# An encoder layer on one core: a snapshot copy moved, one pair's weight sums by DMA, and a written order at the second feed-forward's entry

## The chip, the core and the metric

The kernel runs on one core of a Trainium2 chip. The metric is the device time of one execution in microseconds. TensorE (PE) multiplies matrices, VectorE (DVE) and ScalarE (ACT) work on tiles, GpSimd (POOL) does a little of that and starts some of the transfers, and SyncE (SP) starts the others. Each engine works through its own queue in order and waits where an operand or a buffer is not ready.

## The reference

One layer of an encoder over 512 tokens and 16 meta tokens, 1024 features wide: a feed-forward (FF), a mixer of two branches (a state-space branch and a sparse attention), and a second FF, each with a norm ahead of it and one behind it. `D_FF` is 2816.

```python
def swiglu(x, w_gate, w_up, w_down):
    return (jax.nn.silu(x @ w_gate) * (x @ w_up)) @ w_down
...
        hn = rms_norm(h, ff1_norm_pre[l])
        h = h + 0.5 * rms_norm(swiglu(hn, ff1_w_gate[l], ff1_w_up[l], ff1_w_down[l]), ff1_norm_post[l])
        ...
        merged = g[:, :, 0] * (y_a @ w_branch_a[l]) + g[:, :, 1] * (y_b @ w_branch_b[l])
        h = h + rms_norm(merged @ w_out[l], mix_norm_post[l])
        hn = rms_norm(h, ff2_norm_pre[l])
        h = h + 0.5 * rms_norm(swiglu(hn, ff2_w_gate[l], ff2_w_up[l], ff2_w_down[l]), ff2_norm_post[l])
```

All of it is in float32 outside; the change lies in the last two lines.

## The kernel before

**Products.** Every float32 operand is split into two fp16 halves, high and low: ACT copies the high half (scaled), DVE subtracts it from the operand for the low half. A float32 product is three fp16 matmuls: high by high, high by low, low by high. `split` (L293 on ACT, L295 on DVE) does it for activations; `unit` (L272, L273) for a tile of weights `ws`, whose halves are `wh`.

**Second FF.** The input is `hf`, 8 tiles of 128 features by 512 tokens, both halves. It comes from `wout`, which for each block of 128 tokens multiplies by `w_out` (reading `mg`), norms the rows (tiles `y` of pool W) and in `wout_T` has PE transpose them and `split` write `hf`. Block 0 comes last. The first 256 of the FF's columns are done plainly: `prod(j, 128, SEQ)` for three blocks, and `prod(j, 0, 128)`, 96 matmuls, once block 0's `hf` is there; silu, times up, `split` into `h2f` (L1559, L1560, L295).

The other 2560 columns are worked by class `Strassen` in ten pairs p = 0 to 9 of 128 + 128 columns for gate and for up. A pair is one 2x2 block product in seven block products instead of eight, 24 matmuls of 128x256 each (L139). Its operands are four raw quadrants of the weights (`raw`, 128x4x512 float32, by DMA from a layout that the host made), of which three are split into `wr`, and four sums of quadrants (`sums`, DVE, L122 to L124: slots 0 and 1 are quadrant 3 plus quadrant 0 or 1; slot 2 is slot 0 plus quadrant 1; slot 3 is slot 2 plus quadrant 2), split into `whs` (L112 and L117). The other factor is `hf` itself or one of four combinations of it (`comb` in float32, split into `tops`), made for 128 token columns at a time.

**Order inside a pair.** Products 1, 2, 6, 5, 7 of pair p + 1 and products 4 and 3 of pair p alternate (`run`). Bank Y of a pair collects products 1, 6, 7 and 4 one on another, and between them ACT takes snapshots: p1 after product 1, u2 after 6, u3 after 7 (L155; they read the running sum, so the next product into that bank waits for the copy). `conversions(p)` gives six steps that make the halves of pair p + 2's weights, and `run` calls them by `c()` between the products; the fifth makes the high half `whs` of the second weight and stands ahead of product 7 and of u3.

**What sets the order.** `run` is under a manual schedule: PE, DVE and ACT take its instructions in the written order. The entry ahead of it is ordered by a list scheduler with priorities; `with self.after(marks)` holds what stands in it behind two instructions of `wout`. There pair 0 is loaded and its halves are made. The pools of `wout` close, and those of the second FF (`KP`, `CP`; `tops` lies in `CP`) open behind that; a tile of the new pool is first written when the old pool's readers are through. The constant `ACC` is 0 in the kernel before, and the branch of `load` under it isn't taken.

Of the kernel before, what the change touches and what calls it, by code (L numbers as in the profile page):

```python
# [19 lines left out]
SEQ = 512  # L20
# [53 lines left out]
class Strassen:  # L74
# [14 lines left out]
    def load(self, p):  # L89
        l, nc = self.l, self.l.nc  # L90
        with l.hi():
            for i, w in enumerate(self.w):
                r = l.wst.tile([128, 4, 512], F32, tag="ws", name="raw")
                s = l.SG.tile([128, 4, 512], F32, tag="sums", name="sums", bufs=2)
                if ACC:
                    nc.sync.dma_start(r[:, 0:3], w[p, :, 0:3])
                    nc.sync.dma_start(s[:, 0:2], w[p, :, 3:4].to_broadcast([128, 2, 512]))
                    nc.gpsimd.dma_start(s[:, 0:2], w[p, :, 0:2], accum_op=ADD)
                else:
                    nc.sync.dma_start(r, w[p])  # L100
                self.raw[p, i], self.sums[p, i] = r, s
                self.ops[p, i] = (l.SG.tile([128, 2, 3, 512], F16, tag="wr", name="wr", bufs=4),
                                  l.whl.tile([128, 2, 4, 512], F16, tag="wh", name="whs"))

    def conversions(self, p):

        l, nc = self.l, self.l.nc
        v, s = nc.vector, nc.scalar

        def hi(i, b):  # L110
            src = (self.raw, self.sums)[b][p, i]
            s.activation(self.ops[p, i][b][:, 0], src[:, 0:3] if b == 0 else src, AF.Copy, scale=WS)  # L112

        def lo(i, b):
            src = (self.raw, self.sums)[b][p, i]
            o = self.ops[p, i][b]
            v.scalar_tensor_tensor(o[:, 1], src[:, 0:3] if b == 0 else src, WS, o[:, 0], op0=MUL, op1=SUB)  # L117

        def add(i):
            r, t = self.raw[p, i], self.sums[p, i]  # L120
            if not ACC:
                v.tensor_add(t[:, 0:2], r[:, 3:4].to_broadcast([128, 2, 512]), r[:, 0:2])  # L122
            v.tensor_add(t[:, 2], t[:, 0], r[:, 1])
            v.tensor_add(t[:, 3], t[:, 2], r[:, 2])  # L124
# [16 lines left out]
    def run(self, CP, moving, pair):  # L141
# [16 lines left out]
        for p in range(-1, self.n):  # L158
# [50 lines left out]
            c()  # L209
            if n_:  # L210
                prod(p + 1, 7, Y, "ps", False)
                copy(p + 1, "u3")
                v.scalar_tensor_tensor(st[p + 1, "C"][:, 2], st[p + 1, "u3"], -1.0, by(Z[p + 1]), op0=MUL, op1=SUB)
# [7 lines left out]
class Layer:  # L221
# [1277 lines left out]
    def ff2(self):  # L1499
# [9 lines left out]
        with self.after(self.wout_marks[0]):  # L1509
            sg.load(0)  # L1510
            for f in sg.conversions(0):
                f()
# [11 lines left out]
        for _ in self.wout_T(0):  # L1524
            pass
# [16 lines left out]
        for c in (1, 0):  # L1542
# [3 lines left out]
            for dst, (k, t) in ((b12, (0, 1)), (b22, (1, 1)), (b11, (0, 0)), (b21, (1, 0))):  # L1546
                v.tensor_add(dst, q[k][t][0][:, :, cs], q[k][t][1][:, :, cs])
            v.tensor_sub(t3, b22, b12)
            v.scalar_tensor_tensor(n2, t3, -1.0, b11, op0=MUL, op1=SUB)
            v.scalar_tensor_tensor(t4, n2, -1.0, b21, op0=MUL, op1=SUB)  # L1550
            v.tensor_sub(n1, b11, b12)
            for i, x in ((1, n2), (0, n1), (2, t3), (3, t4)):
                self.split(ops[:, 0, i, :, cs], ops[:, 1, i, :, cs], x)
        for j in range(2):
            prod(j, 0, 128)
        t_ = pair(0, 1)
        for j in range(2):
            sl = CP.tile([128, SEQ], F32, tag="C", name="sl2", bufs=2)
            s.activation(sl, pgs[j][0], AF.Silu, scale=IWS)  # L1559
            v.scalar_tensor_tensor(sl, pgs[j][1], IWS, sl, op0=MUL, op1=MUL)  # L1560
            self.split(t_[:, 0, j], t_[:, 1, j], sl)
        T = lambda i: [ops[:, x, i] for x in range(2)]
        moving = {1: q[0][0], 2: q[1][0], 3: q[1][1], 4: T(3), 5: T(0), 6: T(1), 7: T(2)}
        with self.tc.manual_schedule(engines={mybir.EngineType.PE, mybir.EngineType.DVE, mybir.EngineType.Activation}):
# [93 lines left out]
ACC = 0  # L1658
# [35 lines left out]
```

## Time and profile before

| | |
|---|---|
| runs | 1118.3, 1121.31, 1120.45 us; median 1120.45 us |
| profiled execution | 1121.73 us, span 1120.0 us |
| mean granted clock of PE | 0.979 of full speed |
| PE busy | 1050.3 us (94%), 8382 matmuls |
| DVE, ACT, POOL busy | 759.9 us (68%), 469.5 us (42%), 171.8 us (15%) |
| second FF in the trace | entry 759 to 812 us, loop 812 to 972 us, down projection behind it to the end |

Times are us from the span's start. A matmul's end is modelled, so the steps from start to start are the better measure of a product. The granted clock is a share of 2.4 GHz; 0.5 is 1.2 GHz.

### The profile page before, as it was taken

The numbers are of one execution on the slowest core, as the hardware profiler recorded it, in microseconds if no ns is written. First come the engines' busy times: TensorE is split into PE (matmuls) and PEld (weight loads), VectorE is DVE, ScalarE is ACT, GpSimd is POOL, SyncE is SP. The second block draws the span as 40 slices with busy tenths as digits, with TensorE's granted clock in tenths as the row PEclk, the third lists the DMA queues.
The fourth block names the chain that finished last, engine by engine and source line by source line (L and its number), as shares of the span: only waits on it lengthen the run. The fifth ranks groups of instructions, "written<-read, shape, count | busy, mean of one in ns | idle before, by whom it ended". The sixth has DMA issues, their size and how long they took to land.

```text
span 1120.0 us, 20553 instructions
## 1 busy us (share of the span) xinstructions
PE 1050.3 (94%) x8382; PEld 792.5 (71%) x8382; DVE 759.9 (68%) x1644; ACT 469.5 (42%) x855; POOL 171.8 (15%) x258
## 2 busy tenths in 40 slices
PE   7899999999999999789998899998799899899997
PEld 5788888888888888676654456665688788774443
DVE  7558776668323585599977976599978888754222
ACT  6444333223222155555656453334545445532200
POOL 4400133310000231046431323100000000000000
PEclk9999999999999999999998999999989999999999
DMA  6764445433424045956323124130323323446111
GB/s 193 161 217 135 136 152 168 145 119 111 136 82 118 1 138 170 263 163 171 115 71 110 53 88 163 39 114 38 124 103 114 114 78 111 127 153 225 41 38 38
DMA packets 94479, 135.38 MB, mean 121 GB/s; under 512 B 17336, under 2 KB 69192, under 8 KB 91824
## 3 DMA queue, kind: packets, MB, share of 16 engines
q1 hardware_dynamic: 88704, 119.92, 34.2%
q0 software_dynamic: 5056, 13.08, 4.1%
q8 instruction: 66, 1.08, 0.4%
q10 hardware_dynamic: 624, 1.06, 0.3%
q14 instruction: 29, 0.24, 0.1%
HBM read 118.45 MB, written 19.05 MB: 123 GB/s over the span
## 4 chain that ended last, share of the span: by engine, by line
PE 71%; DVE 14%; DMA 5%; issue 4%; ACT 3%; POOL 1%; SPq 1%; DVEq 0%; ACTq 0%; POOLq 0%
PE psps L316 10%; PE psps L312 10%; PE psps L314 10%; PE psps L139 8%; PE scps L312 6%; PE scps L314 6%; PE scps L316 6%; PE ptps L139 4%; DVE wh L273 3%; DMA ws<-in_w_in_dram 2%; PE avps L139 2%; DMA ws<-in_ff_w_up_dram 1%; DMA X<-in_x_dram 1%; ACT wh L272 1%; PE ptps L316 1%
## 5 line engine op out<-in xcount | busy, mean ns | idle before, releaser
L273 DVE SCALAR_TENSOR_TENSOR wh<-ws,wh 128x512 f16<-128x512 f32 (+2 forms) x184 | 171.9, 972 | 103.1 <-ACT wh L272 102.7
L316 PEld LDWEIGHTS <-wh 128*128 128x128 f16 x1616 | 160.3, 99 | 47.3 <-issue 5.9
L314 PEld LDWEIGHTS <-wh 128*128 128x128 f16 x1616 | 160.6, 99 | 43.2 <-issue 9.7
L312 PEld LDWEIGHTS <-wh 128*128 128x128 f16 x1616 | 160.1, 100 | 42.4 <-issue 6.4
L272 ACT ACTIVATE wh<-ws 128x512 f16<-128x512 f32 (+2 forms) x184 | 138.5, 815 | 120.2 <-PE scps L316 52.3
L312 PE MATMUL psps<-hn,wh 128*128 128x256 f16 (+2 forms) x640 | 166.0, 301 | 3.8 <-DVE kk L297 1.5
L314 PE MATMUL psps<-hn,wh 128*128 128x256 f16 (+2 forms) x640 | 166.4, 301 | 1.1 <-POOL hn L295 0.6
L316 PE MATMUL psps<-hn,wh 128*128 128x256 f16 (+2 forms) x640 | 166.2, 301 | 0.0
L139 PEld LDWEIGHTS <-whs 128*128 128x128 f16 x960 | 93.9, 98 | 14.6 <-issue 3.6
L139 PEld LDWEIGHTS <-wr 128*128 128x128 f16 x720 | 72.5, 101 | 24.7 <-issue 14.3
L312 PE MATMUL scps<-hn,wh 128*128 128x272 f16 (+1 forms) x344 | 69.8, 279 | 4.7 <-ACT sl L507 4.7
L314 PE MATMUL scps<-hn,wh 128*128 128x272 f16 (+1 forms) x344 | 69.4, 278 | 0.0
L316 PE MATMUL scps<-hn,wh 128*128 128x272 f16 (+1 forms) x344 | 69.3, 278 | 0.0
L139 PE MATMUL psps<-tops,whs 128*128 128x256 f16 x480 | 55.8, 273 | 3.2 <-DVE tops L295 1.8
L112 ACT ACTIVATE whs<-sums 128x2048 f16<-128x2048 f32 x20 | 38.1, 1903 | 38.9 <-DVE sums L124 38.9
L117 DVE SCALAR_TENSOR_TENSOR whs<-sums,whs 128x2048 f16<-128x2048 f32 x20 | 45.7, 2287 | 1.6 <-ACT whs L112 1.6
L139 PE MATMUL psps<-tops,wr 128*128 128x256 f16 x240 | 31.7, 295 | 12.5 <-ACT u L155 12.5
L353 POOL DMA_DIRECT2D g_ff_norm_post<-in_ff_norm_post_dram x1 | 0.6, 572 | 269.3 <-ACT sl L175 269.3
L1360 POOL TENSOR_TENSOR BM<-BV,iacc 128x272 f32<-128x272 f32 (+1 forms) x32 | 28.7, 906 | 85.1 <-DVE asm L1366 73.6
L314 PE MATMUL psps<-h,wh 128*128 128x256 f16 (+1 forms) x176 | 41.5, 276 | 0.0
L316 PE MATMUL scps<-h,wh 128*128 128x256 f16 (+1 forms) x176 | 41.5, 276 | 0.0
L312 PE MATMUL psps<-h,wh 128*128 128x256 f16 (+1 forms) x176 | 41.5, 276 | 0.0
(412 smaller groups left out, 2151.1 us busy)
## 6 DMA issues: line engine op xcount, KB each, us to landing
ws<-in_ff_w_down_dram SPq DMA_DIRECT2D x18, 1024.0 KB, 5.1
ws<-in_w_in_dram SPq DMA_DIRECT2D x14, 1024.0 KB, 6.5
ws<-in_ff_w_gate_dram SPq DMA_DIRECT2D x11, 1024.0 KB, 5.4
ws<-in_ff_w_up_dram SPq DMA_DIRECT2D x11, 1024.0 KB, 5.5
raw<-ff_gate_pairs SPq DMA_DIRECT2D x10, 1024.0 KB, 4.8
raw<-ff_up_pairs SPq DMA_DIRECT2D x10, 1024.0 KB, 4.9
ws<-in_w_out_dram SPq DMA_DIRECT2D x4, 1024.0 KB, 5.1
ws<-in_ff_w_down_dram SPq DMA_DIRECT2D x4, 768.0 KB, 4.6
```

Source lines behind the costliest of these rows:

```text
L112: s.activation(self.ops[p, i][b][:, 0], src[:, 0:3] if b == 0 else src, AF.Copy, scale=WS)
L117: v.scalar_tensor_tensor(o[:, 1], src[:, 0:3] if b == 0 else src, WS, o[:, 0], op0=MUL, op1=SUB)
L139: mm(out, a, b[:, kt], start=first and i == kt == x == 0, stop=kt == 3 and x == 2, skip_group_check=True)
L272: nc.scalar.activation(wt[:, 0, ks], st[:, ks], AF.Copy, scale=WS)
L273: nc.vector.scalar_tensor_tensor(wt[:, 1, ks], st[:, ks], WS, wt[:, 0, ks], op0=MUL, op1=SUB)
L312: mm(p, a[0], bh, start=first, stop=False)
L314: mm(p, a[0], bl, start=False, stop=False)
L316: mm(p, a[1], bh, start=False, stop=last)
L353: self.nc.gpsimd.dma_start(dst, bass.AP(tensor=src.tensor, offset=src.offset, ap=[[0, dst.shape[0]], [1, n]]))
L1360: nc.gpsimd.tensor_add(BM[:, :w], self.BV[:, h, NA - w:], madd[:, f:])
```

## The change

Four edits, all around the second FF. First, `load` builds the sums of the pairs under `ACC`, now 1 (pair 0 alone), by DMA: for each of the two weights SP broadcasts quadrant 3 into all four slots of `sums`, POOL starts seven DMAs of 128x512 that add a quadrant to a slot, and `raw` is loaded without quadrant 3. `add` does nothing for that pair. Second, the steps of pair 1's conversions are dealt out anew. Third, `run` puts product 7 and the copy u3 ahead of the fifth `c()`. Fourth, at the entry `load(0)` is no longer held behind `wout`, and pair 0's halves, `wout_T(0)`, the last combinations of block 0, `prod(j, 0, 128)` and the silu stand in written order.

```diff
--- before.py
+++ after.py
@@ -92,36 +92,42 @@
             for i, w in enumerate(self.w):
                 r = l.wst.tile([128, 4, 512], F32, tag="ws", name="raw")
                 s = l.SG.tile([128, 4, 512], F32, tag="sums", name="sums", bufs=2)
-                if ACC:
+                if p < ACC:
+                    nc.sync.dma_start(s, w[p, :, 3:4].to_broadcast([128, 4, 512]))
                     nc.sync.dma_start(r[:, 0:3], w[p, :, 0:3])
-                    nc.sync.dma_start(s[:, 0:2], w[p, :, 3:4].to_broadcast([128, 2, 512]))
-                    nc.gpsimd.dma_start(s[:, 0:2], w[p, :, 0:2], accum_op=ADD)
+                    for c, q in ((0, 0), (1, 1), (2, 0), (3, 0), (2, 1), (3, 1), (3, 2)):
+                        nc.gpsimd.dma_start(s[:, c], w[p, :, q], accum_op=ADD)
                 else:
                     nc.sync.dma_start(r, w[p])
                 self.raw[p, i], self.sums[p, i] = r, s
                 self.ops[p, i] = (l.SG.tile([128, 2, 3, 512], F16, tag="wr", name="wr", bufs=4),
                                   l.whl.tile([128, 2, 4, 512], F16, tag="wh", name="whs"))
 
+    def hi(self, p, i, b):
+
+        src = (self.raw, self.sums)[b][p, i]
+        self.l.nc.scalar.activation(self.ops[p, i][b][:, 0], src[:, 0:3] if b == 0 else src, AF.Copy, scale=WS)
+
+    def lo(self, p, i, b):
+        src = (self.raw, self.sums)[b][p, i]
+        o = self.ops[p, i][b]
+        self.l.nc.vector.scalar_tensor_tensor(o[:, 1], src[:, 0:3] if b == 0 else src, WS, o[:, 0], op0=MUL, op1=SUB)
+
+    def add(self, p, i):
+        if p < ACC:
+            return
+        v = self.l.nc.vector
+        r, t = self.raw[p, i], self.sums[p, i]
+        v.tensor_add(t[:, 0:2], r[:, 3:4].to_broadcast([128, 2, 512]), r[:, 0:2])
+        v.tensor_add(t[:, 2], t[:, 0], r[:, 1])
+        v.tensor_add(t[:, 3], t[:, 2], r[:, 2])
+
     def conversions(self, p):
 
...
+        hi, lo, add = (lambda *a, f=f: f(p, *a) for f in (self.hi, self.lo, self.add))
+        if p == 1:
+            return [lambda: (hi(0, 0), hi(1, 0), lo(0, 0), lo(1, 0)), lambda: (add(0), hi(0, 1)),
+                    lambda: (add(1), hi(1, 1)), lambda: lo(0, 1), lambda: None, lambda: lo(1, 1)]
         return [lambda: (hi(0, 0), add(0)), lambda: (lo(0, 0), hi(1, 0)), lambda: (lo(1, 0), hi(0, 1)),
                 lambda: (lo(0, 1), add(1)), lambda: hi(1, 1), lambda: lo(1, 1)]
 
@@ -206,10 +212,11 @@
                 h = list(h)
                 s.activation(h[0], slf, AF.Copy)
 
-            c()
             if n_:
                 prod(p + 1, 7, Y, "ps", False)
                 copy(p + 1, "u3")
+            c()
+            if n_:
                 v.scalar_tensor_tensor(st[p + 1, "C"][:, 2], st[p + 1, "u3"], -1.0, by(Z[p + 1]), op0=MUL, op1=SUB)
             if p >= 0:
                 v.tensor_sub(h[1], slf, h[0])
@@ -1506,10 +1513,8 @@
         sg = Strassen(self, [I["ff2_%s_pairs" % k] for k in ("gate", "up")])
 
         ug, uu = [self.unit(w, 0, KT, 0, 256, parts=F2P) for w in (wg, wu)]
-        with self.after(self.wout_marks[0]):
-            sg.load(0)
-            for f in sg.conversions(0):
-                f()
+        sg.load(0)
+        manual = lambda: self.tc.manual_schedule(engines={mybir.EngineType.PE, mybir.EngineType.DVE, mybir.EngineType.Activation})
         pgs = [[self.ps("ps"), self.ps("sc")] for j in range(2)]
 
         def prod(j, a, b):
@@ -1521,8 +1526,14 @@
 
         for j in range(2):
             prod(j, 128, SEQ)
-        for _ in self.wout_T(0):
-            pass
+        with self.after(self.wout_marks[0]), manual():
+            for b in range(2):
+                for i in range(2):
+                    sg.hi(0, i, b)
+                    if b == 0:
+                        sg.lo(0, i, b)
+            for _ in self.wout_T(0):
+                pass
         self.sctx.close()
         self.lctx_close()
         self.kctx, self.cctx = ExitStack(), ExitStack()
@@ -1539,29 +1550,52 @@
         q = [[[hf[i][:, 4 * k:4 * k + 4, 256 * t:256 * t + 256] for i in range(2)] for t in range(2)] for k in range(2)]
         R = [KP.tile([128, 4, 256], F32, tag="h", name="raw", bufs=11) for _ in range(4)]
         Tt = [KP.tile([128, 4, 256], F32, tag="h", name="comb", bufs=11) for _ in range(4)]
-        for c in (1, 0):
+        def combine(c, step):
             cs = slice(128 * c, 128 * c + 128)
             b11, b12, b21, b22 = (x[:, :, cs] for x in R)
             n1, n2, t3, t4 = (x[:, :, cs] for x in Tt)
-            for dst, (k, t) in ((b12, (0, 1)), (b22, (1, 1)), (b11, (0, 0)), (b21, (1, 0))):
+
+            def whole(dst, k, t):
                 v.tensor_add(dst, q[k][t][0][:, :, cs], q[k][t][1][:, :, cs])
-            v.tensor_sub(t3, b22, b12)
-            v.scalar_tensor_tensor(n2, t3, -1.0, b11, op0=MUL, op1=SUB)
-            v.scalar_tensor_tensor(t4, n2, -1.0, b21, op0=MUL, op1=SUB)
-            v.tensor_sub(n1, b11, b12)
-            for i, x in ((1, n2), (0, n1), (2, t3), (3, t4)):
+
+            def split(i, x):
                 self.split(ops[:, 0, i, :, cs], ops[:, 1, i, :, cs], x)
-        for j in range(2):
-            prod(j, 0, 128)
+            if step == 0:
+                whole(b12, 0, 1)
+                whole(b22, 1, 1)
+                v.tensor_sub(t3, b22, b12)
+                split(2, t3)
+            if step == 1:
+                whole(b11, 0, 0)
+                v.scalar_tensor_tensor(n2, t3, -1.0, b11, op0=MUL, op1=SUB)
+                split(1, n2)
+            if step == 2:
+                v.tensor_sub(n1, b11, b12)
+                split(0, n1)
+            if step == 3:
+                whole(b21, 1, 0)
+                v.scalar_tensor_tensor(t4, n2, -1.0, b21, op0=MUL, op1=SUB)
+                split(3, t4)
+        for c, step in ((1, 0), (1, 1), (1, 2), (1, 3), (0, 0)):
+            combine(c, step)
         t_ = pair(0, 1)
-        for j in range(2):
-            sl = CP.tile([128, SEQ], F32, tag="C", name="sl2", bufs=2)
-            s.activation(sl, pgs[j][0], AF.Silu, scale=IWS)
-            v.scalar_tensor_tensor(sl, pgs[j][1], IWS, sl, op0=MUL, op1=MUL)
-            self.split(t_[:, 0, j], t_[:, 1, j], sl)
+        with manual():
+            combine(0, 1)
+            sg.lo(0, 0, 1)
+            sg.lo(0, 1, 1)
+            combine(0, 2)
+            for j in range(2):
+                prod(j, 0, 128)
+            sl = [CP.tile([128, SEQ], F32, tag="C", name="sl2", bufs=2) for j in range(2)]
+            for j in range(2):
+                s.activation(sl[j], pgs[j][0], AF.Silu, scale=IWS)
+            combine(0, 3)
+            for j in range(2):
+                v.scalar_tensor_tensor(sl[j], pgs[j][1], IWS, sl[j], op0=MUL, op1=MUL)
+                self.split(t_[:, 0, j], t_[:, 1, j], sl[j])
         T = lambda i: [ops[:, x, i] for x in range(2)]
         moving = {1: q[0][0], 2: q[1][0], 3: q[1][1], 4: T(3), 5: T(0), 6: T(1), 7: T(2)}
-        with self.tc.manual_schedule(engines={mybir.EngineType.PE, mybir.EngineType.DVE, mybir.EngineType.Activation}):
+        with manual():
             sg.run(CP, moving, pair)
         self.cctx.close()
         self.sgctx.close()
@@ -1655,7 +1689,7 @@
 EF = 4
 X1 = 0.4
 X2 = 0.3
-ACC = 0
+ACC = 1
 
 
 def body(tc, I, out, dbg=None):
```

What that makes of the engines' queues is shown at three places; lines are those of either kernel, and the numbers in names tell buffers apart. At the entry, on ACT, from pair 0's first halves to the silu of the first columns, the kernel before has

```order
L112 ACTIVATE wr<-raw 128x1536 x2
L293 ACTIVATE hf<-ptps 128x4x128 x2
L293 ACTIVATE tops<-comb 128x4x128 x5
L1559 ACT_TABLE_LOAD
L1559 ACTIVATE sl_9516<-psps 128x512
L112 ACTIVATE whs<-sums 128x2048
L1559 ACTIVATE sl_9521<-psps 128x512
```

and the changed one

```order
L109 ACTIVATE wr<-raw 128x1536 x2
L300 ACTIVATE tops<-comb 128x4x128 x5
L109 ACTIVATE whs<-sums 128x2048 x2
L300 ACTIVATE hf<-ptps 128x4x128 x2
L300 ACTIVATE tops<-comb 128x4x128 x2
L1591 ACT_TABLE_LOAD
L1591 ACTIVATE sl_9527<-psps 128x512
L1591 ACTIVATE sl_9528<-psps 128x512
```

Two `whs` and all five `tops` now stand ahead of the last block's `hf`, and both `tops` of the last steps ahead of the silu. At the same place POOL, from the last operation of the mixer on, has before

```order
L1360 TENSOR_TENSOR BM<-BV,iacc 128x144
L1369 COPY Pm<-Pt 128x16 x4
L1123 TENSOR_TENSOR T_5720<-T_5720,T_5719 128x4x128 x4
L353 DMA g_ff_norm_post<-in_ff_norm_post_dram 128x1024
L1572 TENSOR_SCALAR g_ff_norm_post<-g_ff_norm_post 128x1024
```

and after

```order
L1130 TENSOR_TENSOR T_5720<-T_5720,T_5719 128x4x128 x4
L99 DMA sums<-ff_gate_pairs 128x512 x4
L99 DMA sums<-ff_up_pairs 128x512 x4
L99 DMA sums<-ff_gate_pairs 128x512 x2
L99 DMA sums<-ff_up_pairs 128x512 x2
L99 DMA sums<-ff_gate_pairs 128x512
L99 DMA sums<-ff_up_pairs 128x512
L360 DMA g_ff_norm_post<-in_ff_norm_post_dram 128x1024
```

The 14 adding DMAs (`L99`) have come in behind the mixer's last operation `T` and ahead of the last norm's load. The second place is ACT in pair 0, from p1 to u3: before

```order
L155 ACTIVATE p1_9563<-psps_9538 128x512
L112 ACTIVATE wr_9531<-raw_9528 128x1536
L112 ACTIVATE wr_9536<-raw_9533 128x1536
L293 ACTIVATE h2f_9515<-sl2_9521 128x512
L293 ACTIVATE tops_9378<-comb_9386 128x4x128
L112 ACTIVATE whs_9532<-sums_9529 128x2048
L155 ACTIVATE u2_9624<-psps_9538 128x512
L112 ACTIVATE whs_9537<-sums_9534 128x2048
L155 ACTIVATE u3_9680<-psps_9538 128x512
```

and after

```order
L161 ACTIVATE p1_9579<-psps_9554 128x512
L109 ACTIVATE wr_9547<-raw_9544 128x1536
L109 ACTIVATE wr_9552<-raw_9549 128x1536
L300 ACTIVATE h2f_9419<-sl2_9527 128x512
L300 ACTIVATE h2f_9419<-sl2_9528 128x512
L109 ACTIVATE whs_9548<-sums_9545 128x2048
L109 ACTIVATE whs_9553<-sums_9550 128x2048
L161 ACTIVATE u2_9644<-psps_9554 128x512
L161 ACTIVATE u3_9696<-psps_9554 128x512
```

Both `whs` of pair 1 now stand ahead of u2; before, one stood ahead of u2 and one ahead of u3. The third place is ACT in the loop, from pair 2's first `whs` to the next pair's p1: before

```order
L112 ACTIVATE whs_9687<-sums_9684 128x2048
L155 ACTIVATE u2_9834<-psps_9693 128x512
L207 ACTIVATE h2f_9867<-sl4_9745 128x1024
L112 ACTIVATE whs_9692<-sums_9689 128x2048
L155 ACTIVATE u3_9894<-psps_9693 128x512
L155 ACTIVATE p1_9933<-psps_9908 128x512
```

and after

```order
L109 ACTIVATE whs_9703<-sums_9700 128x2048
L161 ACTIVATE u2_9850<-psps_9709 128x512
L213 ACTIVATE h2f_9883<-sl4_9761 128x1024
L161 ACTIVATE u3_9909<-psps_9709 128x512
L109 ACTIVATE whs_9708<-sums_9705 128x2048
L161 ACTIVATE p1_9949<-psps_9924 128x512
```

u3 and the second `whs` have changed places, and so in every pair that follows. At the loop's end the two matmuls of the down projection that stood ahead of the last pair's product on PE now stand five products later.

## Rows read from the trace of the kernel before

**Rows 1.** The waits from 770 us on: engine line <- releaser: us in total, times, longest.

```profile
PE psps L139 <- ACT u L155: 13.9, 9, 3.3
```

**Rows 2.** Busy time in stretches: length, busy us by engine (instructions), granted clock, DMA, GB/s.

```profile
core 0: us, PE busy (x) PEld busy (x) DVE busy (x) ACT busy (x) POOL busy (x), PEclk, DMA share, GB/s
853.85:873.80 19.95, 18.49 (x169) 16.42 (x169) 17.15 (x18) 10.17 (x12) 0.00 (x0) 1.00 0.30 106
972.10:1111.60 139.50, 136.74 (x720) 71.16 (x719) 50.47 (x73) 33.08 (x39) 3.37 (x2) 0.99 0.31 106
```

**Rows 3.** The timeline of PE in the loop: start us, us, operation, xcount [idle before <-releaser].

```profile
833.87 2.78 PE L139 MATMUL psps<-tops,wr 128*128 128x256 f16 x24 [0.41 <-ACT u L155]
...
853.82 2.78 PE L139 MATMUL psps<-tops,wr 128*128 128x256 f16 x24 [1.45 <-ACT u L155]
856.44 2.78 PE L139 MATMUL avps<-hf,wr 128*128 128x256 f16 x24
...
974.86 0.90 PE L312 MATMUL scps<-wh,h2f 128*128 128x512 f16 x2 [2.76 <-ACT wh L272]
```

**Rows 4.** The timeline of ACT in the loop.

```profile
851.38 1.91 ACT L112 ACTIVATE whs<-sums 128x2048 f16<-128x2048 f32 x1 [3.52 <-DVE sums L124]
```

**Rows 5.** The timeline of PE at the second FF's entry.

```profile
759.40 0.38 PE L316 MATMUL scps<-wh,mg 128*128 128x512 f16 x1
...
777.14 1.04 PE L1494 MATMUL ptps<-ident,y 128*128 128x128 f32 x8
...
781.45 0.27 PE L314 MATMUL psps<-hf,wh 128*128 128x128 f16 x1 [2.64 <-DVE hf L295]
...
789.35 2.78 PE L139 MATMUL psps<-hf,wr 128*128 128x256 f16 x24
...
796.68 2.67 PE L139 MATMUL psps<-tops,whs 128*128 128x256 f16 x23 [1.82 <-DVE tops L295]
...
812.10 5.28 PE L139 MATMUL psps<-tops,wr 128*128 128x256 f16 x24 [3.32 <-ACT u L155]
```

**Rows 6.** The timeline of ACT at the entry.

```profile
777.78 1.08 ACT L293 ACTIVATE hf<-ptps 128x512 f16<-128x512 f32 x2 [4.00 <-PE ptps L1494]
778.75 2.70 ACT L293 ACTIVATE tops<-comb 128x512 f16<-128x512 f32 x5
781.47 1.28 ACT L1559 ACT_TABLE_LOAD   x1
```

**Rows 7.** The timeline of DVE at the entry.

```profile
789.73 2.28 DVE L117 SCALAR_TENSOR_TENSOR whs<-sums,whs 128x2048 f16<-128x2048 f32 x1
...
801.41 3.42 DVE L117 SCALAR_TENSOR_TENSOR wr<-raw,wr 128x1536 f16<-128x1536 f32 x2
...
806.94 1.22 DVE L122 TENSOR_TENSOR sums<-raw 128x1024 f32<-128x1024 f32 x1
808.20 0.69 DVE L123 TENSOR_TENSOR sums<-sums,raw 128x512 f32<-128x512 f32 x1
```

**Rows 8.** Busy time in short stretches: the granted clock and the DMA's rate (columns of rows 2).

```profile
781.40:786.00 4.60, 4.55 (x44) 4.55 (x44) 4.60 (x8) 1.42 (x3) 0.00 (x0) 0.50 0.00 0
974.86:979.70 4.84, 4.84 (x28) 3.46 (x28) 4.84 (x4) 2.83 (x3) 0.00 (x0) 0.65 0.45 118
796.70:799.30 2.60, 2.60 (x25) 2.33 (x25) 2.60 (x4) 0.00 (x0) 0.00 (x0) 1.00 0.00 0
788.00:789.00 1.00, 1.00 (x22) 1.00 (x19) 1.00 (x3) 1.00 (x3) 0.00 (x0) 1.00 0.99 418
```

**Rows 9.** DMA issues on POOL's queue: xcount, KB each, median us to landing.

```profile
Gd<-B POOLq DMA_DIRECT2D x8, 256.0 KB, 3.5
...
g_mix_norm_post<-in_mix_norm_post_dram POOLq DMA_DIRECT2D x1, 512.0 KB, 5.8
g_ff_norm_pre<-in_ff_norm_pre_dram POOLq DMA_DIRECT2D x1, 512.0 KB, 7.5
```

**Rows 10.** The timeline of POOL after the mixer.

```profile
1004.52 0.57 POOL L353 DMA_DIRECT2D g_ff_norm_post<-in_ff_norm_post_dram  x1 [269.33 <-ACT sl L175]
```

More of the change, by code (lines that the diff above doesn't have):

```diff
@@ L103, in load @@
                                   l.whl.tile([128, 2, 4, 512], F16, tag="wh", name="whs"))
-    def conversions(self, p):
[L107 to L124, printed above, removed]
+    def hi(self, p, i, b):
[13 more added lines that the diff above has]
+        v.tensor_add(t[:, 3], t[:, 2], r[:, 2])
+    def conversions(self, p):
+        hi, lo, add = (lambda *a, f=f: f(p, *a) for f in (self.hi, self.lo, self.add))
+        if p == 1:
+            return [lambda: (hi(0, 0), hi(1, 0), lo(0, 0), lo(1, 0)), lambda: (add(0), hi(0, 1)),
+                    lambda: (add(1), hi(1, 1)), lambda: lo(0, 1), lambda: None, lambda: lo(1, 1)]
         return [lambda: (hi(0, 0), add(0)), lambda: (lo(0, 0), hi(1, 0)), lambda: (lo(1, 0), hi(0, 1)),
```

## Prediction

> **What bounds the kernel now.** I read the page for the shares of the engines, then the waits of the last 350 us by engine, then the timeline of TensorE (PE) through the second feed-forward (FF), and at each gap there the timelines of ScalarE (ACT) and VectorE (DVE). PE is busy for 94% of the span. What it waits for in the second FF is ACT's copy of a product's bank into a snapshot `u` [rows 1]. The gaps recur: the loop over pairs of FF columns has a period of 19.95 us, in which PE is busy for 18.49 and DVE for 17.15 [rows 2]. The gap lies ahead of the product that follows the copy u3, 1.45 us each time [rows 3], because ACT makes the fp16 high half of the weight sums (1.91 us, itself waiting 3.52 us for DVE's sums) just ahead of that copy [rows 4]. Behind the loop PE is busy for 136.74 of 139.50 us, so what the loop's end gains or loses arrives whole at the kernel's end [rows 2]. Some of the clock is lost too: at the loop's end PE waits 2.76 us for a weight half of the down projection [rows 3] and then runs 4.84 us at a mean granted clock of 0.65 [rows 8].
>
> **Loop: the copy u3 ahead of the sums' half.** The copy itself needs only the product before it, so PE goes straight on. A product is 24 matmuls and takes 2.62 us from start to start (853.82 to 856.44 [rows 3]); seven make 18.34 us, against 19.95 before: 1.61 a pair (the wait and 0.16 in which the pipeline refills behind it). There are six such periods from 833.87 on: of the nine waits of 13.9 us in all [rows 1] one is 3.32, one 0.41 and six are 1.45 [rows 3, 5], which leaves 1.4 for one at the entry. 6 x 1.61 = 9.7 us. The first period, 812.10 to 833.87 [rows 3, 5], took 21.77 us, since it began at half clock behind a 3.32 us wait: 21.77 - 18.34 = 3.4 us (that wait is counted with the entry below). At the loop's end two matmuls of the down projection stand ahead of the last pair's product in PE's order before; after, the first of them stands five products further on, and ACT's weight half no longer precedes u3. That takes 2.76 + 0.16 us and the slow stretch, 0.35 x 4.84 = 1.7 us: 4.6 us. **Sum of the loop: 9.7 + 3.4 + 4.6 = 17.7 us gained.** What is late next is DVE, with 17.15 us of work in a period of 18.34: 1.2 us to spare, so I let it not bind. ACT's half behind u3 comes 0.6 us later, and DVE's low half behind it too; its product is over two products away, so that costs nothing.
>
> **Entry: the order of the halves (the change's price).** Before, the copies `hf` of the last token block stand ahead of the five `tops` copies on ACT, and PE has its data at 781.45 [rows 5, 6]. After, ACT has five `tops`, two `whs` and only then `hf`. `tops` lies in a pool that opens when the tiles of y have been read, so it starts at the end of PE's transposes, 777.14 + 1.04 = 778.18 [rows 5]. Then 2.70 for five `tops`, 2 x 1.91 less overlap for `whs`, 0.6 for the first `hf` and 0.6 for DVE's low half make 778.18 + 2.70 + 3.7 + 0.6 + 0.6 = 785.8 [rows 4, 6, 7]: PE starts 4.35 us later. The 96 matmuls of the first columns then take 7.9 us (781.45 to 789.35, of which the first 5.8 run at granted 0.50 [rows 5, 8]): 793.7.
>
> Product 1 of pair 0 takes the bank that the silu reads. On ACT the silu stands behind the `tops` copies of n2 and n1, and n1's sum stands on DVE behind the two low halves `whs` of 2.2 each [rows 7]. In a row from 785.8: DVE hf, sum, combination 1.9 (787.7), ACT `tops` 0.6, DVE's low part 0.7 (789.0), two low halves 4.4 (793.4), n1 0.6, ACT `tops` 0.6, table load 1.28 (795.9) [rows 6], silu 0.6: 796.5. PE waits 2.8 us where it had no wait, and I take its clock to fall, as it did behind waits of 2.64, 2.76 and 3.32 [rows 3, 5, 8]. Product 1 at half clock takes 5.2 us (5.28 for such a product [rows 5]): 801.7; products 2, 6 and 5 end at 809.7.
>
> Product 7 needs the copy u2, and ACT has both sums' halves of pair 1 ahead of it: before, only one. DVE finishes the low halves `wr` at 807.1 (first high half at 803.7, then 3.42 [rows 7]), three 128x512 steps 808.9, then the sums of both weights, 2 x (1.22 + 0.69 + 0.69) and a step between: 814.5. ACT: 1.9 and 0.6 more, 817.0. PE waits 7.3 us; before, it waited 1.4 for u2 (above) and 1.82 for `tops` a little earlier [rows 5]. Product 7 at half clock 5.2, product 1 of the next pair 2.8: the first pass begins at **825.0 instead of 812.10, 12.9 us lost.** The three waits and the slow stretches behind them are all in that number; the DVE sums of pair 0 that go (4.7 us of adds) lie in the stretch that ACT's order now sets, and buy nothing more.
>
> **Sums by DMA.** The two broadcasts wait on SP for the last matmul that reads `mg`, at 759.40 + 0.38 [rows 5]. They move 2 MB; at the 418 GB/s that 16 engines reached [rows 8] that is 5.0 us, with issue and landing some 767 for the second. Each weight then has seven adding DMAs of 256 KB on POOL's queue, 0.57 us of POOL apiece [rows 10], and the last slot gets three, one behind the other's landing. With L for the time from issue to landing, the second weight's sums stand at about 768.5 + 3L. ACT wants them at 782.66, so D = max(0, 768.5 + 3L - 782.66), and the break is at L = 4.7. No row shows an adding DMA. A plain POOL store of 256 KB took 3.5, a load of 512 KB 5.8 and 7.5 [rows 9]. As the add has to read what it adds to, I take more than the store and less than the loads: L = 5, D = 0.8; the ends are 0 (3.5) and 8.3 (7.5). D delays `hf`, so PE, one to one. Nothing below zero is possible here, since earlier sums find ACT still at `tops`. POOL has nothing else queued behind these until 1004, so its waits hold up nobody; SP has only one store and the raw loads of pair 1 behind the broadcasts, and those come some 10 us sooner than before.
>
> By the Trainium skill (DMA: Bandwidth & Descriptors, Anatomy of one DMA — SWDGE (gpsimd) path), a DMA on this path takes about 2.0 us and its bytes over 436 GB/s: an estimate of 2.6 us for 256 KB, with which D would be 0 and the sum 0.8 us less. The stores of 3.5 us [rows 9] are slower than that, and no row here shows an add.
>
> **Sum.** -17.7 + 12.9 + 0.8 = -4.0 us. The profiled execution (1121.73 us, span 1120.0) and the median of the runs, 1120.45, differ by 1.3, 0.1%, so I take the terms over to the median: 1120.45 - 4.0 = **1116.5 us**. A difference under about 0.3%, 3.4 us, can't be told from none by the measurement of this kernel: faster means under 1117.1, slower over 1123.8.
>
> **Rivals.** (1) The adds at half rate: if each has to move its bytes twice, 14 x 256 KB at half of 418 GB/s are 17.6 us, from 765.5 to 783.1, and pair 1's raw loads (2 MB, 5 us) fall into the same stretch: 788.1, D = 5.4, and 1120.45 - 4.8 + 5.4 = 1121.1 us: no difference. For it: 418 GB/s over one us is the most in the stretches I read, and the loads coincide. Against it: between the links of the chain the engines stand idle. The Trainium skill (Collectives: The Full Stack, The bandwidth ceiling: the fold count and why AG ≠ RS ≠ AR) says that an add in the DMA needs two source reads and so halves the rate; the trace neither bears it out nor denies it, for want of an adding DMA.
>
> (2) The other side: the chain of three landings. If each takes as long as the slower 512 KB load, 7.5 us [rows 9], the second weight's sums stand at 791.0, D = 8.3 and the time is 1124.0 us, slower; from L = 7.4 on. For it: each link waits for the one before it to land and for POOL to issue behind the other weight's. Against it: a store of the same size took half of that.
>
> (3) The clock stays up in the 2.8 us wait ahead of product 1. A wait of 1.82 left the granted clock at 1.00, one of 2.64 did not [rows 5, 8]; 2.8 is close to the latter, and my figure for it may be 0.5 off. Product 1 is then 2.6 us shorter: 1113.9 us.
>
> (4) The loop doesn't give its gain: DVE's order, with 1.2 us to spare, makes ACT's second half and with it the next product late, and half of the 9.7 us stays: 1121.3; with all of it 1126.2. Against it: the product that needs the low half has two others ahead of it.
>
> **Chances.** Forecast 0.50, of it 0.37 under 1117.1 (L below about 5.2) and 0.13 within; (1) 0.22, 0.20 within and 0.02 slower; (2) 0.12, 0.10 slower and 0.02 within; (3) 0.08, 0.07 faster and 0.01 within; (4) 0.08, 0.03 within and 0.05 slower. So faster 0.44, same 0.39, slower 0.17. The range goes from 1113.3, below rival 3, to 1124.3, above rival 2; the likeliest case alone spans 1115 to 1118.5. Outside are rival 4 in full and adds slower than any row.
>
> **What would show it.** In the changed kernel's trace: periods of 18.3 us in the loop and no wait for `u` there (rival 4: still over 19); PE's first wait at the entry of about 7.6 us, ended by `hf`, then one of 3 ended by the silu and one of 7 ended by u2; the first pass's start near 825 on the old clock; adding DMAs of about 5 us from issue to landing, with ACT's second `whs` copy within 1 us of its predecessor (rivals 1 and 2: 5 to 9 us behind). The forecast is wrong if the loop's period stays, if the u2 wait is far from 7 us, or if `whs` waits for the sums by more than 3 us.

## The result: slower by 1.3%

The changed kernel takes 1133.68 us (median of 4 runs, 1132.51 to 1135.66) against 1119.45 us for the kernel before (1118.3 to 1121.31): a ratio of 1.0127, 95% interval 1.0104 to 1.0151. The profiled execution took 1132.8 us with a span of 1130.9, 11 us over that of before; that the medians lie 14 us apart is scatter, for before's profiled execution (1121.73) was slower than all four of its runs.

PE's waits from 760 us on in the changed kernel (engine line <- releaser: us in total, times, longest) show what took the place of [rows 1] (a fourth, left out, is 0.5):

```profile
PE psps L319 <- ACT hf L300: 22.7, 1, 22.7
PE psps L145 <- ACT u L161: 7.3, 1, 7.3
PE psps L145 <- ACT sl L1591: 4.1, 1, 4.1
```

All three lie at the entry. The nine waits for `u` are one, and the loop has none: in PE's timeline (start, us, ..., xcount [idle before <-releaser]) pair follows pair in steps of 18.34 us, where [rows 3] had 19.95.

```profile
811.16 5.28 PE L145 MATMUL psps<-hf,wr 128*128 128x256 f16 x24 [4.09 <-ACT sl L1591]
...
831.84 5.28 PE L145 MATMUL psps<-tops,whs 128*128 128x256 f16 x24 [7.32 <-ACT u L161]
...
839.70 2.78 PE L145 MATMUL psps<-tops,wr 128*128 128x256 f16 x24
...
858.04 2.78 PE L145 MATMUL psps<-tops,wr 128*128 128x256 f16 x24
```

The first of these products of the loop starts at 839.70 where before's started at 812.10 [rows 5]. What holds the entry is in ACT's timeline there, against [rows 6]:

```profile
776.98 2.71 ACT L300 ACTIVATE tops<-comb 128x512 f16<-128x512 f32 x5 [5.64 <-PE ptps L1501]
794.82 1.91 ACT L109 ACTIVATE whs<-sums 128x2048 f16<-128x2048 f32 x1 [15.13 <-DMA sums<-ff_gate_pairs]
797.10 1.91 ACT L109 ACTIVATE whs<-sums 128x2048 f16<-128x2048 f32 x1 [0.38 <-DMA sums<-ff_up_pairs]
798.92 1.07 ACT L300 ACTIVATE hf<-ptps 128x512 f16<-128x512 f32 x2
```

ACT is through with `tops` at 779.7 and then stands 15.13 us ahead of the first `whs`, for sums that POOL's adding DMAs have not finished; `hf`, on which PE waits, stands behind. POOL's timeline shows the adds being started, and what each start waited for:

```profile
766.25 3.59 POOL L99 DMA_DIRECT2D sums<-ff_gate_pairs  x4 [32.87 <-DVE y L1484]
768.87 4.48 POOL L99 DMA_DIRECT2D sums<-ff_up_pairs  x4
775.26 0.86 POOL L99 DMA_DIRECT2D sums<-ff_gate_pairs  x1 [1.91 <-DMA sums<-ff_gate_pairs]
776.88 0.86 POOL L99 DMA_DIRECT2D sums<-ff_gate_pairs  x1 [0.76 <-DMA sums<-ff_gate_pairs]
784.50 0.86 POOL L99 DMA_DIRECT2D sums<-ff_up_pairs  x1 [6.76 <-DMA sums<-ff_up_pairs]
787.57 0.86 POOL L99 DMA_DIRECT2D sums<-ff_up_pairs  x1 [2.21 <-DMA sums<-ff_up_pairs]
790.68 0.86 POOL L99 DMA_DIRECT2D sums<-ff_gate_pairs  x1 [2.25 <-DMA sums<-ff_gate_pairs]
793.05 0.86 POOL L99 DMA_DIRECT2D sums<-ff_up_pairs  x1 [1.51 <-DMA sums<-ff_up_pairs]
```

The first eight (one to each slot of both weights) go out one after another and land in that order; the eighth, started at 770.49, took 16.8 us to land by the chain of waits. The chained ones, which add into a slot for the second or third time, wait for an earlier add to land: the two of the first weight start at 775.3 and 776.9, and the last four behind 784. (The releaser of the first line, DVE's `y`, is the nearest event in time; POOL waits there for the broadcast.) The share of the 16 DMA engines in this stretch (columns as in [rows 2]: the last but one is the share, a sum of packet times that can pass 1, the last GB/s) is full for 18 us on end:

```profile
772.00:778.00 6.00, 4.89 (x33) 3.21 (x32) 3.84 (x4) 1.02 (x2) 3.07 (x4) 1.00 1.10 201
778.00:784.00 6.00, 0.00 (x0) 0.00 (x0) 2.74 (x5) 1.69 (x4) 0.00 (x0) 0.60 1.07 312
784.00:790.00 6.00, 0.00 (x0) 0.00 (x0) 0.00 (x0) 0.00 (x0) 1.72 (x2) 0.50 1.07 255
790.00:796.00 6.00, 0.00 (x0) 0.00 (x0) 0.00 (x0) 1.18 (x1) 1.72 (x2) 0.50 0.78 129
```

And the DMA view of 755 to 800 us (queue, kind: packets, MB, share of 16 engines over these 45 us; then issues with KB each and median us to landing), for [rows 9]:

```profile
q0 software_dynamic: 2016, 3.67, 47.8%
q1 hardware_dynamic: 1632, 5.24, 34.6%
...
sums<-ff_up_pairs SPq DMA_DIRECT2D x1, 1024.0 KB, 10.1
raw<-ff_gate_pairs SPq DMA_DIRECT2D x1, 1024.0 KB, 10.0
raw<-ff_up_pairs SPq DMA_DIRECT2D x1, 1024.0 KB, 12.3
```

The 14 adds (q0) hold the 16 engines for 0.478 x 45 = 21.5 us, 1.54 us each, though they are only 3.67 MB. The second broadcast, under way until 768.6, takes 10.1 us, and pair 1's raw loads, started beside the adds, take 10 to 12, against 4.8 for a raw load in the kernel before.

### The profile page after: what moved, and what is told of

Read it like the earlier page. It is cut to its first block, busy times and chain, and to the rows that moved or that the text cites. A ratio compares the mean times of both kernels' runs of the same rounds, so it can differ in the third digit from the quotient of the medians.

```text
span 1130.9 us, 20587 instructions
## 1 busy us (share of the span) xinstructions
PE 1048.3 (93%) x8382; PEld 791.9 (70%) x8382; DVE 757.0 (67%) x1638; ACT 471.4 (42%) x855; POOL 184.6 (16%) x272
## 4 chain that ended last, share of the span: by engine, by line
PE 70%; DVE 13%; DMA 6%; ACT 4%; issue 4%; POOL 2%; SPq 1%; DVEq 0%; ACTq 0%; POOLq 0%
PE psps L323 10%; PE psps L319 10%; PE psps L321 10%; PE psps L145 10%; PE scps L319 6%; PE scps L321 6%; PE scps L323 6%; PE ptps L145 4%; DVE wh L280 2%; DMA sums<-ff_up_pairs 2%; PE avps L145 2%; DMA ws<-in_ff_w_up_dram 1%; DVE iacc L1340 1%; PE ptps L323 1%; PE ptps L321 1%
## 5 line engine op out<-in xcount | busy, mean ns | idle before, releaser
L145 PE MATMUL psps<-tops,whs 128*128 128x256 f16 x480 | 58.2, 280 | 7.3 <-ACT u L161 7.3
L109 ACT ACTIVATE whs<-sums 128x2048 f16<-128x2048 f32 x20 | 38.1, 1905 | 21.9 <-DMA sums<-ff_gate_pairs 15.1
L323 PE MATMUL scps<-h,wh 128*128 128x256 f16 (+1 forms) x176 | 41.5, 276 | 0.0
L323 PE MATMUL psps<-h,wh 128*128 128x256 f16 (+1 forms) x176 | 41.5, 276 | 0.0
L321 PE MATMUL psps<-h,wh 128*128 128x256 f16 (+1 forms) x176 | 41.5, 276 | 0.0
L319 PE MATMUL psps<-h,wh 128*128 128x256 f16 (+1 forms) x176 | 41.5, 276 | 0.0
L321 PE MATMUL scps<-h,wh 128*128 128x256 f16 (+1 forms) x176 | 41.4, 276 | 0.0
```

The lines of the kernel that those rows point to most:

```text
L109: self.l.nc.scalar.activation(self.ops[p, i][b][:, 0], src[:, 0:3] if b == 0 else src, AF.Copy, scale=WS)
L145: mm(out, a, b[:, kt], start=first and i == kt == x == 0, stop=kt == 3 and x == 2, skip_group_check=True)
L319: mm(p, a[0], bh, start=first, stop=False)
L321: mm(p, a[0], bl, start=False, stop=False)
L323: mm(p, a[1], bh, start=False, stop=last)
```

## The experiments

Times are medians; the ratios are to the kernel before, run on the same chip beside each group (1119.6, 1120.1 and 1119.8 us). Where a time is set against the changed kernel's 1133.68 us, the two come from different groups.

**1. The moved copy alone.** The kernel before with the third edit:

```diff
-            c()
             if n_:
                 prod(p + 1, 7, Y, "ps", False)
                 copy(p + 1, "u3")
+            c()
+            if n_:
```

> The kernel before with the third edit alone: product 7 and the copy u3 ahead of the fifth step. If the loop's terms of the prediction are right (17.7 us, of which none needs the new entry), and the entry of before stays as it was, the wait of 3.32 us ahead of 812 goes too, since the same half stood ahead of pair 0's u3: about 20 us less, 1099 us, periods of 18.3 us. If the loop's gain in the changed kernel came from the head start that its late entry gave ACT and DVE, the period stays between 18.5 and 19.5 here and the time is 1105 to 1112.

Measured: 1101.34 us, ratio 0.9838 (0.9814 to 0.9861). PE's timeline:

```profile
796.71 2.67 PE L139 MATMUL psps<-tops,whs 128*128 128x256 f16 x23 [2.95 <-DVE tops L296]
...
808.65 2.78 PE L139 MATMUL psps<-tops,wr 128*128 128x256 f16 x24
...
823.01 2.78 PE L139 MATMUL psps<-tops,whs 128*128 128x256 f16 x24 [1.10 <-ACT u L155]
...
828.25 2.78 PE L139 MATMUL psps<-tops,wr 128*128 128x256 f16 x24
...
846.59 2.78 PE L139 MATMUL psps<-tops,wr 128*128 128x256 f16 x24
```

The wait of 3.32 us at 812 [rows 5] is gone, the loop starts at 808.65, and from 828.25 the period is 18.34 us. The gain of 18.2 us is 2 less than expected: the first pass keeps a wait of 1.10 for u2, and the one for `tops` grew from 1.82 to 2.95. The gain of the loop needs nothing of the other edits. This kernel beats both.

**2. The sums back on DVE.** The changed kernel with `ACC = 0`, and in the written order at the entry:

```diff
             for b in range(2):
                 for i in range(2):
+                    if b == 1:
+                        sg.add(0, i)
                     sg.hi(0, i, b)
```

> The changed kernel with the sums of pair 0 made on DVE again, in the written order just ahead of their high halves; all else as changed. If the time was lost by the adding DMAs (ACT stood 15.1 us ahead of the first whs), the wait of 22.7 us at the entry falls to about 10 and the time to 1117. If it was lost by the written order on ACT and DVE, the time stays above 1128.

Measured: 1116.95 us, ratio 0.9978 (0.9965 to 0.9991). PE's waits:

```profile
PE psps L319 <- ACT hf L300: 9.4, 1, 9.4
PE psps L145 <- ACT u L161: 6.3, 1, 6.3
PE psps L145 <- ACT sl L1593: 3.5, 1, 3.5
```

Of PE's first wait 13.3 us go and of the time 16.7. The sums by DMA alone (broadcasts, adds and the loads beside them) turn a change that gains 2.6 us into one that loses 14. In this run ACT still stands 2.35 us ahead of the second `whs` for DVE's sums, so some 2 us is what earlier sums could have bought. The kernel is 15.6 us slower than that of the first experiment, from the same group: that is the price of the new entry, the second and fourth edits together.

**3. Plain DMAs for the adds.** The changed kernel with

```diff
-                        nc.gpsimd.dma_start(s[:, c], w[p, :, q], accum_op=ADD)
+                        nc.gpsimd.dma_start(s[:, c], w[p, :, q])
```

> The changed kernel with the 14 adding DMAs replaced by plain ones of the same bytes, the same slots, queue and order; the sums of pair 0 are left out by this. If the add itself is dear (each 256 KB holds the DMA engines for 1.4 us and not for 0.65), ACT's whs starts 7 to 10 us sooner and the time is about 1125. If the queue's latency and POOL's issues set it (4 us to landing with nothing beside it, chain of three), whs starts at most 2 us sooner and the time stays at 1132 to 1134.

Measured: 1127.34 us. ACT stands 8.4 us ahead of `whs` instead of 15.1; `whs` starts at 788.6 and not 794.8, 6.2 us sooner and a little less than expected. PE's first wait is 16.1. The DMA view of the same 45 us:

```profile
q0 software_dynamic: 1120, 3.67, 26.3%
```

The same 3.67 MB hold the engines for 0.263 x 45 = 11.8 us instead of 21.5: 0.85 us a transfer instead of 1.54. The add costs 1.8 times a copy. Its packets are smaller, too (2016 of them against 1120), but that isn't what makes it dear: a packet is the piece of a transfer that one engine moves at a time, and in the packet records of the changed kernel's trace a 2 KB packet of an add takes 178 ns (median) and a 2 KB packet of the broadcasts 84, while here a plain packet of 4 KB takes 159. The add isn't all of the delay: 8.4 us are left with plain copies.

**4. Pair 1's raw loads held back.** In `load` of the changed kernel:

```diff
                 else:
+                    if p == 1:
+                        nc.gpsimd.tensor_copy(r[:, 0, 0:1], self.sums[0, i][:, 3, 0:1])
                     nc.sync.dma_start(r, w[p])
```

> The changed kernel with pair 1's two raw loads (2 MB) held back until pair 0's sums have landed: POOL first writes one column of each raw tile from the last slot of the sums. If the adds share full DMA engines with these loads, the sums stand 5 us sooner and the time is about 1129. If each add waits for its own latency and not for bandwidth, the sums come no sooner and the time stays at 1133 or, should the raw loads now be late for ACT, rises to 1136.

Measured: 1128.85 us, as the first theory had it. ACT's timeline:

```profile
789.63 1.91 ACT L111 ACTIVATE whs<-sums 128x2048 f16<-128x2048 f32 x1 [18.58 <-DMA sums<-ff_gate_pairs]
791.44 2.69 ACT L302 ACTIVATE tops<-comb 128x512 f16<-128x512 f32 x5
794.04 1.89 ACT L111 ACTIVATE whs<-sums 128x2048 f16<-128x2048 f32 x1
```

The first `whs` starts 5.2 us sooner, and the second weight's sums land at 792.25 and not 797.1. The adds do share full engines with those loads. PE's first wait falls by less, from 22.7 to 19.9, because the edit also changed ACT's order: the five `tops`, which the changed kernel has behind it before it waits, stand here between the two `whs`.

**5. `hf` first, `whs` behind the silus.** In the changed kernel the written order at the entry is turned:

```diff
-            for b in range(2):
-                for i in range(2):
-                    sg.hi(0, i, b)
-                    if b == 0:
-                        sg.lo(0, i, b)
+            for i in range(2):
+                sg.hi(0, i, 0)
+                sg.lo(0, i, 0)
...
             combine(0, 1)
-            sg.lo(0, 0, 1)
-            sg.lo(0, 1, 1)
...
+            for i in range(2):
+                sg.hi(0, i, 1)
             combine(0, 3)
+            for i in range(2):
+                sg.lo(0, i, 1)
```

> The changed kernel, sums still by adding DMAs, with the written order at the entry turned: the last block's hf ahead of the two whs on ACT, and the whs (high and low) behind the silus. If the late sums cost what they do because hf stands behind whs in ACT's queue, PE's first wait falls from 22.7 to about 1 us, part of the delay comes back as waits ahead of product 6, and the time is about 1121. If the sums' lateness itself is the cost, wherever whs stands, the time stays above 1130.

Measured: 1121.81 us, ratio 1.0014 (0.9997 to 1.0030). PE's waits:

```profile
PE psps L145 <- ACT u L161: 8.8, 1, 8.8
PE psps L145 <- ACT p L161: 6.7, 1, 6.7
PE psps L145 <- ACT sl L1587: 3.1, 1, 3.1
```

The sums are as late as in the changed kernel (`whs` at 793.8 and 796.4), but PE works through the first columns, product 1 and product 2 meanwhile; 12 of the 14 us come back. A part returns as a wait for p1, which now stands behind `whs` on ACT, ahead of product 6 as expected.

**6. Pair 1's old steps.** In `conversions` of the changed kernel:

```diff
-        if p == 1:
+        if p == -1:
```

> The changed kernel with pair 1's six steps dealt out as for the other pairs, so that one whs stands ahead of u2 and not two. The prediction priced the wait for u2 at 7.3 us and the slow product behind it at 2.6. If that is the price of the second edit, the wait goes, some 3 us of it come back in the pair that follows, and the time is about 1129. If DVE's sums are late anyway, the time stays within 1.5 us of 1133.7.

Measured: 1127.49 us, 6.2 less than the changed kernel. PE's timeline:

```profile
813.61 2.78 PE L145 MATMUL psps<-hf,wr 128*128 128x256 f16 x24 [2.65 <-ACT sl L1591]
...
824.09 2.78 PE L145 MATMUL psps<-tops,whs 128*128 128x256 f16 x24
...
845.97 4.45 PE L145 MATMUL psps<-tops,whs 128*128 128x256 f16 x24 [3.37 <-ACT u L161]
...
852.87 2.78 PE L145 MATMUL psps<-tops,wr 128*128 128x256 f16 x24
```

The wait of 7.32 us for u2 ahead of product 7 is gone (824.09), and one of 3.37 has come one pair later (845.97), as expected. From product 1 to the start of the second pass this kernel takes 39.3 us (813.61 to 852.87), the changed one 46.9 (811.16 to 858.04). Of these 7.6 us some 2.7 aren't the edit's: product 1 and the next one run here at full clock behind the silu wait of 2.65, and not behind the 4.09 of the changed kernel. The second edit costs some 5 us.

**7. Plain loads for the broadcasts.** In the changed kernel:

```diff
-                    nc.sync.dma_start(s, w[p, :, 3:4].to_broadcast([128, 4, 512]))
+                    nc.sync.dma_start(s, w[p])
```

> The changed kernel with SP's two broadcasts of quadrant 3 replaced by plain loads of all four quadrants into the same slots: 1 MB each as before, in rows of 8 KB; the sums of pair 0 are wrong by this. The broadcasts took 8 to 10 us where a raw load of 1 MB takes 4.9. If the small rows (2 KB) or the fourfold reading make them slow, they land by 763 to 764, the adds start 3 us sooner and the time is about 1131. If POOL's queue or another load beside them sets their landing, nothing moves.

Measured: 1129.51 us, near the 1131 of the first theory, with single runs from 1126.1 to 1131.9. The load of the second weight lands after 7.0 us, not 10.1, POOL starts its adds at 762.75 instead of 766.25, and PE's first wait is 20.0.

```profile
sums<-ff_up_pairs SPq DMA_DIRECT2D x1, 1024.0 KB, 7.0
```

Which of the two did it, the rows of 2 KB or one quadrant read four times, this leaves open. The profiled execution is the fastest of the four, and part of its gain is the clock: product 1 runs at full clock behind a silu wait of 2.80 us.

```profile
807.74 2.78 PE L145 MATMUL psps<-hf,wr 128*128 128x256 f16 x24 [2.80 <-ACT sl L1591]
```

**8. Pair 0's sums on POOL.** The kernel of the first experiment with

```diff
         def add(i):
+            v = nc.gpsimd if p < 1 else nc.vector
             r, t = self.raw[p, i], self.sums[p, i]
```

> The kernel before with the third edit (u3 ahead of the fifth step) and pair 0's sums added on POOL, which is idle there, in place of DVE; no DMA adds. From the first experiment's 1101.3: DVE loses 5 us of adds between 774 and 788, POOL makes them in about 10 us from 760 on, and the two whs go ahead of hf without a wait. The waits of 3.0 for tops and 2.5 for u2 go, the one for hf grows from 2.6 to 4.2: 1098. If POOL is slower than the 1.27 us per 128x512 of its adds in the mixer, or slows DVE beside it, the time is 1101 or more.

Measured: 1104.9 us, ratio 0.9868 (0.9851 to 0.9886), 3.6 more than the first experiment: the second branch. POOL's timeline, and then DVE's beside it:

```profile
760.39 5.11 POOL L123 TENSOR_TENSOR sums<-raw 128x1024 f32<-128x1024 f32 x2 [24.73 <-DVE y L1486]
765.47 2.94 POOL L124 TENSOR_TENSOR sums<-sums,raw 128x512 f32<-128x512 f32 x2
768.36 3.46 POOL L125 TENSOR_TENSOR sums<-sums,raw 128x512 f32<-128x512 f32 x2
```

```profile
767.20 1.22 DVE L335 SCALAR_TENSOR_TENSOR sm<-sm 128x1 f32<-128x1 f32 x1
768.34 0.68 DVE L1549 TENSOR_TENSOR raw<-hf 128x512 f32<-128x512 f16 x1
768.94 3.42 DVE L1550 TENSOR_TENSOR comb<-raw 128x512 f32<-128x512 f32 x2
```

POOL was nearly as quick as I took it to be (11.4 us, not 10). But while it adds, single operations of DVE take long: 1.22 us for 128x1 and 1.7 apiece for two 128x512, where 0.2 and 0.68 are usual (and 0.68 is seen beside POOL too). Behind 772, when POOL is through, the same operations take the usual time again. The last block's norm on DVE and with it `hf` come some 7 us later than in the first experiment.

**9. The three together.** Experiments 3, 4 and 7 in one kernel (the expectation counts them as the third, fourth and eighth).

> The changed kernel with the edits of the third, fourth and eighth run of this study together: plain DMAs for the adds, pair 1's raw loads held back, plain loads for the broadcasts (the sums of pair 0 are wrong by this). Singly they took 6.3, 4.8 and 4.2 us off, and 6.6, 2.8 and 2.7 off PE's first wait of 22.7. If the lateness is bandwidth in these three parts, they add up: a first wait of 8 to 11 us, 1118. If a fixed latency of the chain of three stays beneath them, the first wait stays above 13 us and the time above 1122.

Measured: 1119.84 us, ratio 1.0007 (0.9992 to 1.0022), and

```profile
PE psps L321 <- ACT hf L302: 11.1, 1, 11.1
```

The three shares add up, near enough: what they take off singly sums to 12.1 of the 22.7 us, and 10.6 were to be left. As in experiment 4, the five `tops` stand between the two `whs` here, so the sums' own lateness has fallen by more than PE's wait.

**10. Without the chain.** The changed kernel with the first eight adds alone:

```diff
-                    for c, q in ((0, 0), (1, 1), (2, 0), (3, 0), (2, 1), (3, 1), (3, 2)):
+                    for c, q in ((0, 0), (1, 1), (2, 0), (3, 0)):
```

> The changed kernel with the first eight adding DMAs alone, one to a slot; the six that wait for an earlier one to land are left out, and with them part of the sums. In the changed kernel the eighth landed at 787.3 and the whs started at 794.8 and 797.1. If the chained six are what comes on top of a full queue, the second whs starts at about 787.5, PE's first wait falls by 9 us and the time to 1124. If the eight alone are slower or faster than in the changed kernel (because the six share their engines), the second whs moves by more than 2 us against that.

Measured: 1123.92 us. ACT's timeline:

```profile
775.68 1.91 ACT L109 ACTIVATE whs<-sums 128x2048 f16<-128x2048 f32 x1 [5.34 <-DMA sums<-ff_gate_pairs]
...
786.36 1.91 ACT L109 ACTIVATE whs<-sums 128x2048 f16<-128x2048 f32 x1 [8.77 <-DMA sums<-ff_up_pairs]
```

PE's first wait is 12.9. Eight adds need until 786 by themselves (the eighth again lands after 16.9 us); the six chained ones put another 10 us on top. In this run ACT has both `whs` and `hf` ahead of the five `tops`, which doesn't touch the landing of the sums.

## Why the prediction was wrong

**The loop, 17.7 us: right.** From the start of the product at 839.70 to PE's last matmul (1121.12 + 0.38) the changed kernel takes 281.8 us, the kernel before 299.5 (812.10 to 1111.6 [rows 2, 5]): 17.7. The periods are 18.34, the wait for the down projection's half is gone, DVE did not bind (rival 4 falls), and the first experiment gives the same period without the other edits.

**The entry's order, 12.9 us: right but for 1.3.** The waits were to be 2.8 for the silu and 7.3 for u2; they are 4.09 and 7.32, each followed by a product of 5.28 us. So in this trace the clock fell behind the silu wait: in the window from 811 to 816 us the granted clock is 0.50, as in [rows 8] behind 2.64:

```profile
811.00:816.00 5.00, 4.84 (x23) 3.34 (x23) 1.55 (x3) 1.12 (x3) 0.00 (x0) 0.50 0.01 3
```

That doesn't refute rival 3, whose wait of 2.8 us isn't the 4.09 measured. In experiment 7 the silu wait was 2.80 and left the granted clock at 1.00; so did 2.65 in experiment 6 and, at the entry of experiment 1, 2.95. The length of the wait alone, by which the prediction chose, doesn't settle it, and that the clock fell as forecast was partly luck. Experiment 6 puts the two `whs` ahead of u2 at some 5 us.

**The sums by DMA, D = 0.8: this step failed.** It was "the second weight's sums stand at about 768.5 + 3L", with L = 5. The sums stood at 797.1, so that 3L came to 28.6 us and not 15. PE's first wait was to be 8.4 us (the 7.6 among the prediction's signs leaves D out) and is 22.66: D is the 15.13 us that ACT stands ahead of `whs`, and not 0.8. As the landing of a lone add, L was not far off: with little beside them the last two landed in 4.1 and 4.0 us (from 790.68 to 794.8 and from 793.05 to 797.1). What the formula lacks is that the eight adds ahead of the chain are not eight landings side by side. They go through the same 16 engines one after another, 1.54 us each, and these are full: with the adds go the broadcasts, until 768.6, and the raw loads that the change itself brings forward into this stretch. The eighth add took 16.8 us to land, not 5: with the raw loads held back it took 11.8 (experiment 4), near the 12.3 us for which eight adds hold the engines. The formula counted three landings, and the first of them was worth more than three.

**Rival 1 had the mechanism and too small a price.** It said that the adds run at half rate and meet pair 1's loads, 1121.1 us with a chance of 0.22. Experiment 3 shows the rate (1.54 against 0.85 us), and experiment 4 the meeting (5 us). Its delay of the sums, 5.4 us, is 9.7 short of the 15.1 measured, for three reasons: 1.25 us an add instead of 1.54 (17.6 against 21.5 in all); the broadcasts at 418 GB/s, where they landed only after 8 to 10 us (experiment 7: 2.7 us of PE's first wait); and it let the work end when the engines have moved the bytes, whereas the last links of the chain come one by one behind it with the engines part idle (a share of 0.78 in the last window above; experiment 10). By the Trainium skill (Collectives: The Full Stack, The bandwidth ceiling: the fold count and why AG ≠ RS ≠ AR) the add of a ReduceScatter needs two source reads and so runs at half the rate of a copy. The ratio here is 1.8 for a transfer and 2.1 for a packet of 2 KB, so the trace agrees. The estimate of 2.6 us for 256 KB by the Trainium skill (DMA: Bandwidth & Descriptors, Anatomy of one DMA — SWDGE (gpsimd) path) is not borne out by the adds, the quickest of which took 4.0 us; the quickest plain one took 3.2 (experiment 3).

**Rival 2** came nearer to the result than rival 1, at 1124.0 us, and named the chain, but by luck: its 7.5 us fits no link. The first was 16.8, the other two 5.2 and 4.0.

**What hid the cost** was a landing time read from transfers that went nearly alone [rows 9] and used for 14 at once. The path was seen: `hf` stands behind `whs` in ACT's written order, so whatever is late there is late for PE one to one. That was said in the prediction, and experiment 5 shows it by taking the order apart: the same late sums, 12 us less. But what the adds, the broadcasts and the raw loads do to each other was priced in rival 1 alone, not in the forecast. The sum of the terms as measured: 13.7 forecast for the entry, and 15.2 more (14.3 for D, 1.3 for the silu, 0.4 less for the first columns), less 17.7 for the loop: +11.2, against +10.9 between the spans.

## What to carry to other kernels

Price a batch of DMAs by the time for which it holds the engines, with all that is moved into the same stretch, and then add one landing for each link that must wait for another; a landing time taken from a lone transfer is the least, not the typical. An add in the DMA costs nearly two copies. Where an operand comes late, look at what stands behind its first user in that engine's order before paying to make it earlier: in this kernel a snapshot copy moved by two lines gained 18 us, and a whole apparatus for earlier sums cost 16.7, where some 2 were to be had.

## What the runs showed of the hardware that I had not expected

- An adding DMA of 256 KB holds the 16 engines for 1.54 us and a plain one of the same bytes for 0.85; POOL takes 0.86 us to start the one and 0.54 the other. Beside either, raw loads of 1 MB took 10 to 12 us (10.0 and 12.3 beside the adds, 10.1 and 11.9 beside plain DMAs).
- A broadcast of one 256 KB quadrant into 1 MB took up to 10.1 us, a plain load of 1 MB in its place 7.0.
- While POOL adds float32 tiles (experiment 8), some operations of DVE on 128x1 take 1.22 us and some on 128x512 1.7 us; others beside them keep their usual time. An idle POOL isn't a free one if DVE is on the path.
- PE's granted clock was 1.00 behind waits of 2.65, 2.80 and 2.95 us (experiments 6, 7 and 1) and 0.50 behind one of 2.64 (before) and one of 4.09 (the changed kernel).
